# Moving one convolution tile behind the triangular inverse, on memory that the recurrence's preparation leaves

## Chip, cores and metric

The kernel runs on one core of one Trainium2 chip. The metric is the device time in microseconds (us) of one execution. Engines are called as the profile calls them: PE (TensorE), PEld (its weight loads), DVE (VectorE), ACT (ScalarE), POOL (GpSimd), SP (SyncE, which here issues nearly all DMAs).

## What is computed

One decoder layer over 1024 tokens of width 1024, in float32: a mixer, a cross-attention into 256 memory tokens and a SwiGLU, each between two RMS norms and added to the residual stream. The change lies in the mixer. One input projection feeds two groups of 512 channels; their outputs go through one output projection:

```python
p = rms_norm(x, g[0]) @ w_in_first
y_conv = conformer_conv(p[..., :2 * D_CONV], ...)   # gate, 31 taps per channel, layer norm, silu
y_rwkv, v_first = rwkv7_mix(p[..., 2 * D_CONV:], ...)
y = jnp.concatenate([y_conv, y_rwkv], axis=-1) @ w_out
```

The RWKV-7 group is a recurrence over tokens with a 64x64 state per head. The kernel runs it in chunks of 64 tokens, for which it inverts a triangular 64x64 matrix per chunk and head.

## The kernel before

**Tiling.** The tokens go in two blocks of 512 (b = 0 and 1), the 512 channels of a group in four tiles of 128 (j = 0 to 3, or four head pairs hp = 0 to 3). Each float32 matmul is done as three (`mm3`, L195 to L197) on operands split into a high and a low part. Weights are loaded raw (`wraw`), and ACT and DVE split them (`split`, L172 `whi` and L173 `wlo`); there are four raw buffers, and two each of `whi` and `wlo` at this point of the kernel.

**Stages around the change, block 0.** In the order of the code in `run`:

- `rwkv_prep(0)`, the preparation of the recurrence: decays, keys, products (`psg`, masked on DVE into `am`, L528), and bonus and gate (`bvd`, `gnd`), for head pairs 0 to 3. Its tiles are in the pool `prep0`. Its second half is asked for behind the rest of block 0's input projection.
- The memory tokens' norm (`normed(self.mem, ...)`: `xt`, the transposes `pstr`, and `ahi` and `alo`, L278 and L279). Its transposes take their PSUM from the ring `pd` of four tiles, the one from which the projections' sums `psf` come too.
- `rwkv_values(0)`, and the first panels of block 1's input projection.
- `conv_taps(0, ..., range(2))`: the convolution's tiles 0 and 1. One tile is a load `hin` (SP), one ACT activation for tap 0 and a bias (L351), and 30 dependent DVE instructions on one accumulator (L353), below called taps.
- `rwkv_inverse(0)`: loads `At`, then 31 steps of two dependent DVE instructions each (L619, L620), a way through DRAM, and small matmuls on PE.
- `rwkv_chain(0)`, the recurrence over eight chunks. Beside it lie more projection panels and the maps of the cross-attention (`memory_maps`), woven with the convolution's tiles 2 and 3 and its layer norm.
- `mix_out(0)`, the output projection, which loads what convolution and recurrence have written to DRAM (`araw<-yd`).

The order in the code is not the order on the engines. The kernel is built with `TileContext(nc, schedule_with_timeline_sim=True)`: a planner lays the instructions out on each engine when the kernel is compiled; what is asked for earlier has precedence, and what comes later fills in where it is ready. On the chip each engine then works through its list in order.

**Memory.** Pools are stacked from two sides, L and R. Tiles of one tag share a number of buffers. A pool that is opened where another was closed waits tile by tile (`reuse_waits="tile"`): a tile waits for the tiles whose place it takes. Before the change, both accumulators lie in the pool `conv0` on R, which has been open since the start, so that nothing holds them back. The pool `prep0` is the lowest on L behind the constants and weights; in it the tag `p2` (eight buffers of 2304 bytes a partition) is asked for first. An accumulator takes 2048 bytes. The memory map of the compiled kernel before shows the first `p2` buffer at the bottom of the pool; the last tile that it holds is `k` of head pair 3, which `factors(3)` reads for the last time in L514. `At` begins 8192 bytes above the bottom, behind `TT`, and its 4096 bytes reach into the buffer that holds `v` of head pair 3 last.

```python
for k in range(1, CONVW):
    nc.vector.scalar_tensor_tensor(out=a, in0=h[:, k:k + TB], scalar=w(k), in1=a, ...)
...
for t in range(31):
    ...
    nc.vector.tensor_tensor(out=w, in0=a, in1=c, op=ALU.mult)
    nc.vector.tensor_tensor(out=u, in0=u, in1=w, op=ALU.add)
```

Of the kernel before, what the change touches and what calls it, by code (L numbers as in the profile page):

```python
# [50 lines left out]
def weave(main, side, rate):  # L51

    lag = 0.0
    for us in main:
        yield us
        lag += us * rate
        while lag > 0.0:
            lag -= next(side, 1e9)
    drain(side)


def drain(*gens):
    for g in gens:
        for _ in g:
            pass


class Trunk:
# [883 lines left out]
    def run(self):  # L952
        tc = self.tc
        L, R = "left", "right"
        opened = {}

        def push(name, side):
            opened[name] = tc.tile_pool(name=name, bufs=1, side=side, reuse_waits="tile")
            return opened[name].__enter__()

        def pop(*names):
            for n in names:
                opened.pop(n).__exit__(None, None, None)
# [12 lines left out]
        kp = push("conv0", R)  # L976
# [18 lines left out]
        mk = push("mk", R)  # L995
        self.xn = 2
        self.xp = push("xb", R)
        drain(prep)
        pop("prep0")
        mT = self.pairs(mk, MEM, "m")  # L1000
        self.normed(self.mem, 0, (0, 2), mT, "g_mem", 2, (self.pd, "d"))
        self.rwkv_values(0, None)
        drain(self.w_in_block(1, h1, ev, conv_cols))

        acc = []
        drain(self.conv_taps(0, kp, kp, acc, range(2)))
        tp = push("tt0", L)
        TT = tp.tile([P, NCH * HP, CH], F32, tag="TT", name="TT")
        pp = push("inv0", L)
        self.rwkv_inverse(0, pp, TT)  # L1010
        pop("inv0")
        kv = push("kv", R)
        ka = push("conv0b", L)
# [5 lines left out]
        def conv_rest():  # L1019
            yield from self.conv_taps(0, kp, ka, acc, range(2, 4))  # L1020
            yield from self.conv_norm(0, kp, acc)
        main = chain(self.w_in_block(1, h1, ev, mix_cols[:3]), maps)
        drain(weave(main, conv_rest(), 1.0))
        pop("mix0", "gn0", "conv0b", "tt0", "kv", "xb", "mk", "conv0")
        self.filler = self.w_in_block(1, h1, ev, mix_cols[3:])

        yp = push("y0", L)
# [7 lines left out]
        kp = push("conv1", R)  # L1035
# [6 lines left out]
        acc = []  # L1042
# [20 lines left out]
        kp = push("conv1b", R)  # L1063
        acc = [kp.tile([P, TB], F32, tag="acc%d" % j, name="acc") for j in range(2)]
# [90 lines left out]
```

## Time and profile before

| | |
|---|---|
| median of 3 runs | 1613.07 us (1611.14 to 1615.81) |
| profiled execution, its own time | 1606.14 us |
| its span, first to last instruction | 1604.4 us |
| mean granted TensorE clock | 0.975 of full speed |
| PE busy | 1521.0 us (95%) |
| DVE busy | 1067.6 us (67%) |
| ACT busy | 685.9 us (43%) |

The profiled execution has a span of 1604.4 us and 1.74 us around it. Busy shares are means over stages with different limits. The PE is nearly always busy, so what counts is where it isn't, or where its clock is low. Times in the rows are microseconds from the start of the span.

### The profile page before, as it was taken

How to read it: one execution, taken by the hardware profiler on the slowest of the kernel's cores; microseconds unless marked ns; L12 is line 12 of the kernel's file. 1: busy time of each engine (PE TensorE's matmuls, PEld its weight loads, DVE VectorE, ACT ScalarE, POOL GpSimd, SP SyncE). 2: the span in 40 equal slices, each digit the busy share in tenths (PEclk: the TensorE clock that was granted, in tenths of full speed). 3: DMA queues.
4: the chain of work that ended last, by engine and by line, in shares of the span. 5: the costliest groups of instructions: out<-in, count | busy, mean ns of one | idle time of the engine just before them, and what ended most of it. 6: DMA issues, size and time to landing. Idle time of an engine off the chain costs nothing.

```text
span 1604.4 us, 22598 instructions
## 1 busy us (share of the span) xinstructions
PE 1521.0 (95%) x8688; PEld 1243.1 (77%) x8688; DVE 1067.6 (67%) x1704; ACT 685.9 (43%) x1064; POOL 57.3 (4%) x102
## 2 busy tenths in 40 slices
PE   6999699999796899899999999999999999999997
PEld 5878578888575787687888777788887888888886
DVE  6699958799689555678685997646548534444445
ACT  6554423566833344554223446434444332222222
POOL 2000000000002001000100000000002000000000
PEclk9999699999998899899999999999999999999999
DMA  6555677788646235365955444535347533333321
GB/s 219 185 168 171 197 212 250 223 284 264 217 158 203 92 99 174 99 180 172 255 160 160 148 144 149 187 119 183 92 132 244 175 102 95 94 104 92 96 88 53
DMA packets 176219, 258.41 MB, mean 161 GB/s; under 512 B 68976, under 2 KB 110064, under 8 KB 176112
## 3 DMA queue, kind: packets, MB, share of 16 engines
q1 hardware_dynamic: 175152, 256.13, 51.6%
q8 instruction: 68, 1.11, 0.3%
q10 hardware_dynamic: 960, 0.85, 0.2%
q14 instruction: 39, 0.32, 0.1%
HBM read 197.10 MB, written 59.83 MB: 160 GB/s over the span
## 4 chain that ended last, share of the span: by engine, by line
PE 78%; DVE 10%; ACT 5%; DMA 3%; issue 3%; POOL 0%; SPq 0%; DVEq 0%; ACTq 0%; POOLq 0%
PE psf L195 14%; PE psf L197 14%; PE psf L196 14%; PE pst L195 9%; PE pst L196 9%; PE pst L197 9%; DVE acc L353 4%; DVE wlo L173 1%; PE psg L525 1%; PE pstr L275 1%; ACT whi L172 1%; DVE ya L770 1%; DMA xt<-in_x_dram 1%; PE pss L702 1%; PE psq L692 1%
## 5 line engine op out<-in xcount | busy, mean ns | idle before, releaser
L172 ACT CAST whi<-wraw 128x1024 fp32r<-128x1024 f32 x256 | 268.1, 1050 | 561.9 <-PE psf L196 242.2
L173 DVE TENSOR_TENSOR wlo<-wraw,whi 128x1024 fp32r<-128x1024 f32 x256 | 312.3, 1221 | 262.4 <-ACT whi L172 258.1
L195 PE MATMUL psf<-ahi,whi 128*128 128x512 f32 (+1 forms) x1200 | 457.4, 383 | 15.6 <-ACT whi L172 10.3
L197 PE MATMUL psf<-ahi,wlo 128*128 128x512 f32 (+1 forms) x1200 | 456.8, 381 | 1.3 <-DVE wlo L173 1.2
L196 PE MATMUL psf<-alo,whi 128*128 128x512 f32 (+1 forms) x1200 | 457.3, 381 | 0.0
L195 PEld LDWEIGHTS psf<-ahi,whi 128*128 128x128 f32 x1200 | 228.6, 191 | 61.8 <-ACT whi L172 13.0
L197 PEld LDWEIGHTS psf<-ahi,wlo 128*128 128x128 f32 x1200 | 228.3, 190 | 44.6 <-DVE wlo L173 2.5
L196 PEld LDWEIGHTS psf<-alo,whi 128*128 128x128 f32 x1200 | 228.7, 191 | 41.3 <-issue 0.2
L353 DVE SCALAR_TENSOR_TENSOR acc<-hin,cols,acc 128x512 f32<-128x512 f32 x240 | 170.4, 742 | 5.8 <-ACT acc L351 5.6
L195 PE MATMUL pst<-whi,ahi 128*128 128x512 f32 x384 | 142.9, 399 | 11.3 <-ACT ahi L172 7.4
L196 PE MATMUL pst<-wlo,ahi 128*128 128x512 f32 x384 | 151.0, 395 | 0.1
L197 PE MATMUL pst<-whi,alo 128*128 128x512 f32 x384 | 146.0, 393 | 0.0
L196 PE MATMUL pst<-wlo,fhi 128*128 128x512 f32 x352 | 137.6, 392 | 0.0
L197 PE MATMUL pst<-whi,flo 128*128 128x512 f32 x352 | 134.4, 390 | 0.0
L195 PE MATMUL pst<-whi,fhi 128*128 128x512 f32 x352 | 133.8, 393 | 0.0
L195 PEld LDWEIGHTS pst<-whi,ahi 128*128 128x128 f32 x384 | 72.9, 190 | 28.4 <-ACT ahi L172 7.9
L196 PEld LDWEIGHTS pst<-wlo,ahi 128*128 128x128 f32 x384 | 73.2, 191 | 15.2 <-DVE wlo L173 0.6
L235 POOL TENSOR_TENSOR rstd<-rstd,mhalf 128x1 f32<-128x1 f32 x50 | 39.8, 804 | 1220.4 <-DVE rstd L234 1211.2
L197 PEld LDWEIGHTS pst<-whi,alo 128*128 128x128 f32 x384 | 71.9, 189 | 14.5
L919 DVE TENSOR_TENSOR ya<-pst,ya 128x512 f32<-128x512 f32 x80 | 53.9, 686 | 35.6 <-PE pst L197 35.4
L937 DVE SCALAR_TENSOR_TENSOR ftg<-ftg,psf 128x512 f32<-128x512 f32 x44 | 30.2, 686 | 70.7 <-PE psf L197 70.5
L196 PEld LDWEIGHTS pst<-wlo,fhi 128*128 128x128 f32 x352 | 66.1, 188 | 14.2 <-DVE wlo L173 0.4
(244 smaller groups left out, 1699.5 us busy)
## 6 DMA issues: line engine op xcount, KB each, us to landing
wraw<-in_w_gu_dram SPq DMA_DIRECT2D x88, 512.0 KB, 3.7
wraw<-in_w_in_dram SPq DMA_DIRECT2D x44, 512.0 KB, 4.3
wraw<-in_w_down_dram SPq DMA_DIRECT2D x44, 512.0 KB, 3.7
am<-amd SPq DMA_DIRECT2D x16, 512.0 KB, 5.7
wraw<-in_wkv_dram SPq DMA_DIRECT2D x16, 512.0 KB, 4.7
wraw<-in_w_out_dram SPq DMA_DIRECT2D x16, 512.0 KB, 4.4
wraw<-gd SPq DMA_DIRECT2D x16, 512.0 KB, 4.1
wraw<-vwd SPq DMA_DIRECT2D x16, 512.0 KB, 3.6
```

What stands on the lines that cost most here:

```text
L172: self.nc.scalar.copy(out=hi, in_=src)
L173: self.nc.vector.tensor_tensor(out=lo, in0=src, in1=hi.bitcast(F32), op=ALU.subtract)
L195: mm(ps, w[0], x[0], start=start, stop=False)
L196: mm(ps, w[0], x[1], start=False, stop=False)
L197: mm(ps, w[1], x[0], start=False, stop=stop)
L235: nc.gpsimd.tensor_tensor(r, r, self.mhalf, op=ALU.pow)
L275: nc.tensor.transpose(ps[:, t * P:(t + 1) * P], xt[:, k * P:(k + 1) * P], self.ident)
L353: nc.vector.scalar_tensor_tensor(out=a, in0=h[:, k:k + TB], scalar=w(k), in1=a, op0=ALU.mult, op1=ALU.add)
L525: nc.tensor.matmul(pg[g][:, i, :], bk[half[g], c + i, :], aq[half[g], :, c + i, :], start=True, stop=True)
L692: nc.tensor.matmul(pq[rows, j, :], S[rows, j, :], qt[rows, j, :], start=True, stop=True)
L919: nc.vector.tensor_tensor(out=y, in0=ps, in1=y, op=ALU.add)
L937: nc.vector.scalar_tensor_tensor(out=tg, in0=tg, scalar=0.5, in1=pu, op0=ALU.mult, op1=ALU.mult)
```

## The change

Tile 1's accumulator leaves the pool `conv0` (R) for a pool of its own, `conv0q`, which is opened on L when `prep0` has been closed. It takes the lowest 2048 bytes that `prep0` had. The pools that follow on L (`tt0`, `inv0`, later `conv0b`, `gn0`, `mix0`) move up by 2048 bytes, those on R that lie above `conv0` move by 2048 bytes too. Tile 1's load, its activation and its 30 taps are asked for behind `rwkv_inverse(0)` instead of ahead of it. The number of instructions stays as it is.

```diff
         drain(prep)
         pop("prep0")
+
+        kq = push("conv0q", L)
         mT = self.pairs(mk, MEM, "m")
...
         acc = []
-        drain(self.conv_taps(0, kp, kp, acc, range(2)))
+        drain(self.conv_taps(0, kp, kp, acc, range(1)))
         tp = push("tt0", L)
         TT = tp.tile([P, NCH * HP, CH], F32, tag="TT", name="TT")
         pp = push("inv0", L)
         self.rwkv_inverse(0, pp, TT)
+        drain(self.conv_taps(0, kp, kq, acc, range(1, 2)))
         pop("inv0")
...
-        pop("mix0", "gn0", "conv0b", "tt0", "kv", "xb", "mk", "conv0")
+        pop("mix0", "gn0", "conv0b", "tt0", "conv0q", "kv", "xb", "mk", "conv0")
```

## Rows read from the trace of the kernel before

**Rows 1.** The page's slices: busy tenths in 40 equal slices of the span.
```profile
PE   6999699999796899899999999999999999999997
DVE  6699958799689555678685997646548534444445
```
**Rows 2.** Windows: stretch, its length, busy us of each engine, granted clock, DMA share.
```profile
163.00:188.00 25.00, 15.52 (x59) 10.44 (x60) 24.96 (x44) 12.28 (x23) 1.74 (x4) 0.53 0.70 207
188.00:204.00 16.00, 16.00 (x83) 12.57 (x84) 15.87 (x26) 5.83 (x9) 0.52 (x1) 0.89 0.51 157
204.00:236.00 32.00, 32.00 (x181) 25.54 (x181) 15.90 (x23) 9.04 (x13) 3.80 (x6) 1.00 0.78 213
236.00:276.00 40.00, 40.00 (x182) 33.11 (x181) 36.07 (x91) 12.48 (x17) 0.00 (x0) 1.00 0.79 250
296.00:390.00 94.00, 85.36 (x936) 76.26 (x936) 85.35 (x130) 59.50 (x99) 0.00 (x0) 1.00 0.83 265
390.00:445.00 55.00, 42.65 (x353) 34.48 (x352) 41.93 (x69) 43.43 (x66) 0.00 (x0) 0.90 0.71 227
```
**Rows 3.** Waits of PE, 100 to 220: total us, times, longest.
```profile
PE psg L525 <- ACT cs L490: 5.8, 1, 5.8
PE psf L195 <- DVE alo L279: 3.7, 1, 3.7
```
**Rows 4.** Windows of the taps (L353) alone: length, DVE busy (instructions), clock.
```profile
100.00:142.00 42.00, 21.62 (x31) 1.00 0.66 198
142.00:163.00 21.00, 9.92 (x14) 1.00 0.52 164
163.00:188.00 25.00, 8.67 (x12) 0.53 0.70 207
188.00:196.00 8.00, 2.29 (x4) 0.77 0.41 120
```
**Rows 5.** Timeline of ACT at 156 and of DVE at 186: start, length, instruction.
```profile
156.74 1.28 ACT L241 ACT_TABLE_LOAD   x1 [2.58 <-DVE rn L471]
...
185.88 0.74 DVE L353 SCALAR_TENSOR_TENSOR acc<-hin,cols,acc 128x512 f32<-128x512 f32 x1
186.55 0.87 DVE L279 SCALAR_TENSOR_TENSOR alo<-pstr,cols,ahi 128x256 fp32r<-128x256 f32 x2
```
**Rows 6.** Timeline of SP's queue: loads of tiles 2 and 3.
```profile
188.10 0.32 SPq L347 DMA_DIRECT2D hin<-hd  x1
...
195.03 0.32 SPq L347 DMA_DIRECT2D hin<-hd  x1
```
**Rows 7.** Timeline of DVE: last read of `k` of head pair 3.
```profile
203.68 0.75 DVE L514 SCALAR_TENSOR_TENSOR r<-r,cols,k 128x512 f32<-128x512 f32 x1
```
**Rows 8.** Waits of SP's queue, 200 to 300.
```profile
SPq L601 <- DMA bvd<-v: 4.7, 1, 4.7
```
**Rows 9.** Timeline of DVE in the inverse: first step, some steps, last step.
```profile
236.66 0.19 DVE L619 TENSOR_TENSOR tm<-At,Tt 128x31 f32<-128x31 f32 x1 [4.04 <-DMA At<-sc]
...
245.89 0.40 DVE L619 TENSOR_TENSOR tm<-At,Tt 128x231 f32<-128x231 f32 x1
246.32 0.40 DVE L620 TENSOR_TENSOR Tt<-Tt,tm 128x231 f32<-128x231 f32 x1
246.64 0.68 DVE L327 SCALAR_TENSOR_TENSOR evh<-tg,psf 128x512 f32<-128x512 f32 x1
247.24 0.40 DVE L619 TENSOR_TENSOR tm<-At,Tt 128x240 f32<-128x240 f32 x1
...
274.78 0.22 DVE L620 TENSOR_TENSOR Tt<-Tt,tm 128x31 f32<-128x31 f32 x1
```
**Rows 10.** Timeline of DVE at the recurrence's end: last state, last output.
```profile
426.97 0.42 DVE L704 TENSOR_TENSOR Sn<-pss,Sn 128x256 f32<-128x256 f32 x1
...
444.13 0.69 DVE L740 TENSOR_TENSOR Y<-Y,bv 128x512 f32<-128x512 f32 x1
```
**Rows 11.** Waits of PE, 440 to 470.
```profile
PE pst L195 <- ACT ahi L172: 7.4, 1, 7.4
```

## The prediction

> **What bounds the kernel now.** I began with the page's slices. The PE is full nearly everywhere, so a change to DVE work can pay only where the PE is not full: here in slice 5 (160 to 200 us) and in slices 11 and 13 [rows 1]. The accumulators of the change belong to the first of these places, so I cut it with windows. From 163 to 188 the PE is busy 15.52 of 25 us, at a mean clock of 0.53, while DVE is busy 24.96 of 25 [rows 2]. The PE's list of waits says what it lacks there: once ACT (5.8 us, `cs`) and once DVE (3.7 us, `alo` of the memory norm, which holds the ring of sums that the next projection panel needs) [rows 3]. So in this stretch DVE sets the pace. From 204 to 236 the picture is turned round: the PE is full, and DVE is busy 15.90 of 32 us. From 236 to 276, while the inverse runs, it is busy 36.07 of 40, and beside the recurrence (296 to 390) 85.35 of 94 [rows 2].
>
> Who fills DVE from 163 to 188? The taps alone take 8.67 us of it, 12 instructions; 14 lie from 142 to 163, 4 from 188 to 196 [rows 4]. They are the lowest in precedence of all that is asked for there, and the stretch is where work is late. Both tiles run alternately: tile 2's load, which needs tile 0's `hin`, goes out at 188.10, and tile 3's, which needs tile 1's, at 195.03, so both end within 7 us of each other [rows 6]. One tap in front of the instruction on which the PE waits can be seen: at 185.88, ahead of `alo` at 186.55 [rows 5].
>
> Behind this stretch two things run. The PE's stream of panels goes on full until the recurrence begins. The recurrence ends later than the stream has work for: its last state comes at 426.97, its last output at 444.13 [rows 10], the PE is busy 42.65 of 55 us from 390 to 445 [rows 2], and then it waits 7.4 us for the recurrence's part of `mix_out`'s input [rows 11]. So a gain ahead of the inverse counts for the total only as far as it reaches the recurrence's end.
>
> **The change part by part.** Durations are those of the profiled execution.
>
> *Taps taken out of the full stretch.* With tile 1 away, tile 0's 30 taps take the slots alone. By 142 there were 31 [rows 4], so tile 0 should be done at about 145, and from 163 to the release of the PE 11 taps are gone (12 less the one behind 186.55): 11 x 8.67/12 = 7.9 us. Bounds: if tile 0, whose taps wait for one another, spreads over the same stretch and keeps half the slots, 4.0 us; if the taps ahead of `rn` that delay ACT's table load at 156.74 (it idled 2.58 us for it [rows 5]) go as well, 7.9 + 2.2 (three taps of 0.72) = 10.1. I take 7.9.
>
> *The same from 188 to 204.* Four taps (2.29 us [rows 4]) and the sum of the two accumulators leave a DVE that is busy 15.87 of 16 [rows 2], ahead of the last factors of the preparation. The PE is full there too, so between 0 and 2.3 us; I take 1.5.
>
> *When tile 1 can start.* Its accumulator takes the bottom of `prep0`, so it waits for `k` of head pair 3, last read at 203.68 [rows 7] (about 194 after the gains above), and not for the preparation's last stores: `At`, which lies on `v`'s buffer, waited for that one's store (`bvd`) 4.7 us [rows 8], as it will after the change, since `At` moved by 2048 bytes still covers it. `hin` has a buffer free from the start.
>
> *Taps put into the idle stretch.* From `k`'s last read to the inverse's first step DVE has 32 - 15.90 = 16.1 us idle [rows 2], room for 22 taps of 0.72. They hide under a full PE, but some stand in front of preparation work on the way to `At`: some nine DVE instructions of the last head pairs, half of which meet a tap half done, 9 x 0.5 x 0.36 = 1.6 us. Bounds 0 and 3.2; I take 1.5.
>
> *Taps left for the inverse.* Eight remain. The inverse's two instructions per step depend on each other, and the planner puts whatever is ready between them. What one costs can be read at 246: from 245.89 to 246.32 the pitch is 0.43, so the next step was due at 246.75; with `evh` (0.68) in between it came at 247.24, 0.49 late [rows 9]. A tap (0.74, as at 185.88 [rows 5]) would cost 0.55, eight 4.4 us. But DVE idles 40 - 36.07 = 3.9 us in that stretch [rows 2], in which some hide. Bounds 0.5 and 4.4; I take 2. [...]
>
> *Nothing else.* The load, activation and taps are the same in number. SP's queue has tile 1's load behind the inverse's in precedence, but it needs nothing that is late. The moved pools at 204 and later stand on tiles that were freed earlier than they are asked for, `At` aside. Tiles 2 and 3 wait for the inverse's memory as before.
>
> *Sum.* At the inverse's end: -7.9 - 1.5 + 1.5 + 2.0 = -5.9 us. The recurrence and `mix_out` behind it move by the same amount, since the PE's stream, which moves by some 8, stays ahead. The profiled execution would come to 1606.14 - 5.9 = 1600.2 us (span 1598.5). The runs' median lies 6.9 us above this execution; I put the difference on it: 1613.07 - 5.9 = 1607.2 us.
>
> **The rivals.**
>
> *The stall stays.* ACT's chain and the transposes at half clock, not DVE's queue, set the PE's restart at 187: then taking the taps out leaves DVE idle and the PE waiting. For it: the longest wait in [rows 3] is on ACT, and the PE itself works at clock 0.53 there [rows 2]. Against it: DVE idles 0.04 of 25 us, and at the restart it is DVE that the PE waits for. At most ACT's 2.2 us would be won, against 1.5 + 2 lost later: 1613 + 1.3, about 1614 us, or the gain goes into the PE's idle time ahead of `mix_out`; no change.
>
> *The inverse pays (the slower one).* Tile 1's taps have precedence over block 1's later panels and alternate with the inverse. If they start late, as they would if the accumulator were held until the store that `At` awaits, only about 5 us x 1/0.72 = 6 fit ahead of the first step at 236.66 [rows 9], and 24 lie in the inverse: 24 x 0.55 = 13.2 us, and the 1.5 in the preparation, against the 9.4 won: +5.3, so 1618.4 us. It decides from (9.4 - 1.5)/0.55 = 14 taps in the inverse on. For it: the alternation is seen at 246 [rows 9]; against it: `k`'s last read at 203.68 is 33 us ahead of the inverse.
>
> *The clock recovers.* The PE drops from 2.4 to about 1.2 GHz in the stall (granted 0.53, and 0.89 from 188 to 204 [rows 2]) after it has waited. If the shorter stall keeps it up, 16 x 0.11 = 1.8 us of the restart come back, and at most half of the 15.52 us busy (7.3 at 0.53): -7.7 to -13.2, so 1605 to 1600 us. In the Trainium skill, page "TensorE: Matmul & The Clock Gate", section "Terms", the penalty is the throttled time times the share of pulses withheld. By that the two stretches would hold 25 x 0.47 + 16 x 0.11 = 13.5 us to win, which is more than the rows allow, since the PE stood still for 9.5 us of them.
>
> *The change doesn't do what it says:* the planner already spaces both tiles by what is ready, and tile 0 fills all slots that tile 1 leaves. Then 0 us.
>
> **How the numbers follow.** What a measurement of this kernel can tell from no change is 0.3%, here 4.8 us. Chances: the sum as forecast 0.55 (its own range, by the bounds of the first term, is -2.0 to -8.1, 1605 to 1611 us; 0.43 of it beyond 0.3%, 0.12 within); the clock's extra gain 0.05; the stall stays 0.20; the change doesn't do it 0.03; the inverse pays 0.17. That makes faster 0.48, same 0.35, slower 0.17. The range goes from 1600 (the gains' upper bounds, 10.1 + 2.3 with nothing paid back but 0.5, are 11.9 us, and with the clock's least 13.7) up to 1616.5, where part of the slower case begins; about 1 in 10 is left out on each side.
>
> **What would show it.** Right: no taps between 150 and 190; PE busy more than 18 of the 25 us there, its restart (first `psf` behind the memory norm) near 179 instead of 187; `k`'s last read near 194 and tile 1's taps from then to about 235; the inverse's last step near 269 instead of 275, the last output near 438. Wrong: taps of tile 0 up to 180 (the first term), a restart that doesn't move (the stall stays), more than 14 taps between the inverse's first and last step (the slower case), or an inverse that ends at 269 and a last output still at 444, in which case the gain is lost beside the recurrence, whose DVE is nearly full.

## The result, and the profile after

The changed kernel is slower: 1627.34 us (median of 4 runs) against 1614.39 us (median of 4 runs of the kernel before), ratio 1.0088, 95% interval 1.0071 to 1.0105 (ratios, here and below, are those on record; the quotient of two medians can differ from them by up to 0.0008). Three executions among the runs below, with a mean granted clock of 0.65 to 0.74 and 19 to 37% more time, are left out of medians and ratios. The profiled execution of the changed kernel took 1626.74 us with a span of 1625.0 us, so it stands near its median. The one of before (1606.14 us) lies 8 us below its own median. Differences between the two traces therefore come out larger (20.6 us of span) than those between the medians (13 us).

The windows of [rows 2], and behind them the taps alone (their line, L353; length, DVE busy, clock), whose first three stretches are those of [rows 4]:
```profile
163.00:188.00 25.00, 19.81 (x86) 14.42 (x86) 22.05 (x36) 16.61 (x28) 2.68 (x5) 0.73 0.62 189
188.00:204.00 16.00, 16.00 (x95) 12.98 (x94) 11.40 (x16) 5.69 (x8) 0.00 (x0) 1.00 0.65 172
204.00:236.00 32.00, 32.00 (x178) 26.36 (x177) 21.07 (x37) 8.34 (x11) 4.66 (x6) 1.00 0.93 258
...
390.00:445.00 55.00, 38.29 (x381) 28.76 (x375) 40.24 (x73) 30.97 (x49) 0.00 (x0) 0.74 0.45 144
```
```profile
100.00:142.00 42.00, 19.94 (x27) 1.00 0.69 208
142.00:163.00 21.00, 2.53 (x4) 1.00 0.66 207
163.00:188.00 25.00, 0.00 (x0) 0.73 0.62 189
...
204.00:228.00 24.00, 2.24 (x3) 1.00 0.92 258
228.00:304.00 76.00, 20.19 (x27) 1.00 0.76 242
```
The reader is to see two halves. Up to 204 the change does what was forecast: no tap stands between 163 and 188, the PE is busy 19.81 us there instead of 15.52 [rows 2], and at a higher clock (0.73, not 0.53). From 204 on it doesn't: ahead of the inverse DVE is filled little more than before (13.55 of the 24 us from 204 to 228, 12.01 before; the 21.07 of 32 in the window above hold the first steps of the inverse), 3 taps lie ahead of the inverse and 27 in it.

The timeline says how that comes. First the stretch in which tile 1 might have started and the one in which it did (DVE and ACT), then the inverse's first and last instruction and, from its middle, one step with all that lies between its two instructions:
```profile
195.37 0.75 DVE L514 SCALAR_TENSOR_TENSOR r<-r,cols,k 128x512 f32<-128x512 f32 x1
...
220.23 0.69 ACT L554 ACTIVATE cs<-pspr,cols 128x512 f32<-128x512 f32 x1 [2.27 <-DVE v L552]
220.81 0.81 ACT L351 ACTIVATE acc<-hin,convb,cols 128x512 f32<-128x512 f32 x1
...
221.65 0.75 DVE L353 SCALAR_TENSOR_TENSOR acc<-hin,cols,acc 128x512 f32<-128x512 f32 x1
...
228.38 0.19 DVE L619 TENSOR_TENSOR tm<-At,Tt 128x31 f32<-128x31 f32 x1
...
241.98 0.32 DVE L619 TENSOR_TENSOR tm<-At,Tt 128x156 f32<-128x156 f32 x1
242.22 1.22 DVE L173 TENSOR_TENSOR wlo<-wraw,whi 128x1024 fp32r<-128x1024 f32 x1
243.35 0.74 DVE L309 SCALAR_TENSOR_TENSOR evq<-psf,cols,evq 128x511 f32<-128x511 f32 x1
244.01 0.74 DVE L353 SCALAR_TENSOR_TENSOR acc<-hin,cols,acc 128x512 f32<-128x512 f32 x1
244.67 0.22 DVE L312 SCALAR_TENSOR_TENSOR evq<-carry,cols,evq 128x1 f32<-128x1 f32 x1
244.80 0.32 DVE L620 TENSOR_TENSOR Tt<-Tt,tm 128x156 f32<-128x156 f32 x1
...
303.47 0.21 DVE L620 TENSOR_TENSOR Tt<-Tt,tm 128x31 f32<-128x31 f32 x1
```
`k` is read for the last time at 195.37, 8.3 us earlier than before [rows 7]. Tile 1's activation comes 25 us later, directly behind `L554`, the preparation's last instruction on ACT, and with no wait listed in front of it: the trace shows nothing on the chip that held it, it stands there in ACT's program. The inverse then starts 8.3 us earlier than before [rows 9] and ends 28.7 us later (303.47 against 274.78): it takes 75 us instead of 38. In the step shown, the second instruction starts 2.82 us behind the first (0.43 in the step of [rows 9] with nothing between), and only one of the four instructions between them is a tap.

What lies in DVE between the inverse's first and last step, by line; first the kernel before, then the changed one (busy us, mean ns; the last column is idle time before them):
```profile
L619 DVE TENSOR_TENSOR tm<-At,Tt 128x31 f32<-128x31 f32 (+15 forms) x31 | 10.6, 341 | 4.7 <-DMA At<-sc 4.0
...
L173 DVE TENSOR_TENSOR wlo<-wraw,whi 128x1024 fp32r<-128x1024 f32 x7 | 8.6, 1222 | 1.5 <-ACT whi L172 1.3
```
```profile
L173 DVE TENSOR_TENSOR wlo<-wraw,whi 128x1024 fp32r<-128x1024 f32 x19 | 23.2, 1224 | 3.9 <-ACT whi L172 3.9
L353 DVE SCALAR_TENSOR_TENSOR acc<-hin,cols,acc 128x512 f32<-128x512 f32 x27 | 20.2, 748 | 0.0
L619 DVE TENSOR_TENSOR tm<-At,Tt 128x31 f32<-128x31 f32 (+15 forms) x31 | 10.6, 341 | 0.4
...
L832 DVE TENSOR_TENSOR kvl<-psf,kvh 128x256 fp32r<-128x256 f32 x7 | 2.9, 418 | 0.0
```
The inverse's own work is the same (31 steps; 10.6 us for the first instructions of all of them). The taps bring 20.2 us. Beside them 19 splits of weight panels (`wlo`) lie in the stretch instead of 7, which is 14.6 us more, and 7 evacuations of the memory's projections (`kvl`, 2.9 us, the last of them directly behind the last step) that before came behind it. The PE runs on with its panels while the inverse lasts, and each panel asks DVE for a split and evacuations: the longer the inverse takes, the more of them it has to let through.

Behind the inverse the delay goes on. The recurrence's end, for [rows 10], and the PE's wait ahead of `mix_out`, for [rows 11]:
```profile
448.70 0.42 DVE L704 TENSOR_TENSOR Sn<-pss,Sn 128x256 f32<-128x256 f32 x1
...
464.12 0.69 DVE L740 TENSOR_TENSOR Y<-Y,bv 128x512 f32<-128x512 f32 x1
```
```profile
PE pst L195 <- ACT ahi L172: 5.9, 1, 5.9
```
The last state is 21.7 us later than before, the last output 20.0 us (464.12 against 444.13), and the span 20.6 us longer. The whole loss is there when the recurrence ends; behind it nothing is added, and the PE's wait ahead of `mix_out` is no longer than before (5.9 us, 7.4 in [rows 11]). The PE has run out of other work by then: from 390 to 445 it is busy 38.29 us (42.65 before) at a clock of 0.74.

### The profile page after: what moved, and what is told of

The parts are those of the page before. It is cut to its first block, busy times and chain, and to the rows that moved or that the text cites. A ratio compares the mean times of both kernels' runs of the same rounds, so it can differ in the third digit from the quotient of the medians.

```text
span 1625.0 us, 22615 instructions
## 1 busy us (share of the span) xinstructions
PE 1527.2 (94%) x8688; PEld 1249.2 (77%) x8688; DVE 1069.1 (66%) x1704; ACT 686.3 (42%) x1064; POOL 57.8 (4%) x102
## 4 chain that ended last, share of the span: by engine, by line
PE 79%; DVE 9%; ACT 4%; DMA 4%; issue 3%; SPq 0%; POOL 0%; DVEq 0%; ACTq 0%; POOLq 0%
PE psf L195 15%; PE psf L197 14%; PE psf L196 14%; PE pst L195 9%; PE pst L196 9%; PE pst L197 9%; DVE acc L353 3%; PE psg L525 1%; DVE wlo L173 1%; PE pstr L275 1%; DVE ya L770 1%; PE pspr L439 1%; DMA vwd<-evw 1%; DMA xt<-in_x_dram 1%; ACT whi L172 1%
## 5 line engine op out<-in xcount | busy, mean ns | idle before, releaser
L353 DVE SCALAR_TENSOR_TENSOR acc<-hin,cols,acc 128x512 f32<-128x512 f32 x240 | 173.1, 749 | 12.1 <-ACT acc L351 11.4
L196 PEld LDWEIGHTS pst<-wlo,fhi 128*128 128x128 f32 x352 | 66.1, 188 | 14.2 <-DVE wlo L173 0.4
```

What stands on the lines that cost most here:

```text
L196: mm(ps, w[0], x[1], start=False, stop=False)
```

## The experiments

Each was timed beside the kernel before on the same chip; ratios are to that. Its median was 1610.12 us beside the runs of the order alone, of no taps, of the first hold and of tile 1 beside the recurrence; 1610.93 beside the memory alone, half the taps, the second hold and GpSimd; and 1611.20 beside the three with late taps. "Inverse" is from the start of its first step on DVE to that of its last, "last output" the last `Y` of the first block's recurrence, both in the profiled execution (before: 38.1 us and 444.13). Two executions of one program differ in these places too: the first run below has the program of the kernel before, and its last output came at 451.53. Differences of some us in the last output prove nothing by themselves; the medians decide.

**The order alone.** The tile is asked for behind the inverse, but its accumulator stays in `conv0`.
```
-        drain(self.conv_taps(0, kp, kp, acc, range(2)))
+        drain(self.conv_taps(0, kp, kp, acc, range(1)))
...
         self.rwkv_inverse(0, pp, TT)
+        drain(self.conv_taps(0, kp, kp, acc, range(1, 2)))
```


> Only the order is changed: tile 1 is asked for behind the inverse, but its accumulator stays in the pool conv0, which is open from the start. Theory (late memory: the accumulator on the preparation's memory is held until the preparation's last instructions are out, so that 27 of its taps fall into the inverse): the taps run as before, alternating with tile 0's, all 60 done before the inverse begins; the inverse takes 38 us and the time is that of before, 1614 us within 5. Rival (order: whoever is asked for behind the inverse alternates with it, wherever its memory lies): some 27 taps in the inverse, 75 us for it, and about 1627 us.

Measured: 1610.72 us, ratio 1.0008 (0.999 to 1.0025); inverse 37.7 us, without a tap; the PE is busy 14.78 of 25 us from 163 to 188. The planner puts all taps where they were: on DVE and ACT the trace has the same instructions in the same order as the kernel before, from the first to the last. The order does nothing by itself. As one program in two executions, the two traces also show how far such traces lie apart: this one's granted clock was 0.85 from 296 to 330 (1.00 in the trace before) and its last output 7.4 us later.

**The memory alone.** The accumulator lies in the recurrence's memory, but the tile is asked for ahead of the inverse, as before.
```
         drain(self.conv_taps(0, kp, kp, acc, range(1)))
+        drain(self.conv_taps(0, kp, kq, acc, range(1, 2)))
...
         self.rwkv_inverse(0, pp, TT)
-        drain(self.conv_taps(0, kp, kq, acc, range(1, 2)))
```


> Tile 1's accumulator lies in the recurrence's memory as in the change, but the tile is asked for ahead of the inverse, as before. Theory (the memory decides, the order does nothing): tile 1's activation comes behind the preparation's last instructions (near 221), some 27 taps lie between the inverse's first and last step, 1625 to 1630 us, as the change. Rival (both edits are needed): tile 1 starts near 195, at most 10 taps in the inverse, 1605 to 1613 us.

Measured: 1626.99 us, ratio 1.0094 (1.0078 to 1.0109); inverse 75.5 us, last output 465.72. ACT's timeline in this run:
```profile
220.67 0.69 ACT L554 ACTIVATE cs<-pspr,cols 128x512 f32<-128x512 f32 x1 [2.27 <-DVE v L552]
221.25 0.81 ACT L351 ACTIVATE acc<-hin,convb,cols 128x512 f32<-128x512 f32 x1
```
The activation stands behind the same instruction as in the changed kernel, although the tile is asked for earlier; in all, PE, DVE and ACT have the same instructions in the same order as in the changed kernel, so that this is a second measurement of its program (16 us slower than the kernel before). With the run before, this settles it: the memory makes the loss and sets the start; the order has no part in it.

**No taps.** The changed kernel without tile 1's 30 taps (its convolution is left out).
```
-            for k in range(1, CONVW):
+            for k in range(1, 1 if (b, j) == (0, 1) else CONVW):
```


> The changed kernel without tile 1's 30 taps (load and activation stay; the convolution of 128 channels in block 0 is left out but for its first tap). Theory: what is lost lies in these taps alone, so the inverse is back at about 38 us with 7 splits of weights in it, the PE's restart stays at its early place, the recurrence begins some 8 us earlier than before, and the time is 1614 - 6 = 1608 us (1602 to 1612). Rival (moved pools: the shift by 2048 bytes makes new waits): the loss stays, 1620 us or more. Rival (nothing to win: the early restart of the PE is given back at the recurrence): 1614 us.

Measured: 1600.14 us, ratio 0.9944 (0.9929 to 0.996); PE 19.76 of 25 us from 163 to 188, inverse 40.0 us, last output 441.67. That is below the forecast (1602 to 1612). The moved pools do no harm, and freeing the full stretch is worth some 9 us if the taps cost nothing elsewhere. From here to the changed kernel it is 0.0144 in the ratio, 23 us, for 30 taps of 0.75 us on DVE (22 us). The inverse is longer by 35 us (75.1 against 40.0). Without the taps the planner also laid out other instructions in another order, so the comparison holds more than the taps' removal; no run keeps the rest in place.

**Half the taps.** The changed kernel with tile 1's taps 16 to 30 left out.
```
-            for k in range(1, CONVW):
+            for k in range(1, 16 if (b, j) == (0, 1) else CONVW):
```


> The change with 15 of tile 1's 30 taps left out (its convolution is cut short there); 3 taps ahead of the inverse and 12 in it, against 27 and none. Theory (a tap costs its 0.75 us divided by the share of DVE that the panels' splits and evacuations leave, about 0.6, so 1.25 us): the inverse takes 40 + 12 x 1.25 = 55 us, the whole 1610 to 1616 us, half way between the change and the one with no taps of tile 1. Prediction's price (0.55 us per tap): the inverse 40 + 6.6 = 47 us, 1603 to 1607 us.

Measured: 1608.35 us, ratio 0.999 (0.9977 to 1.0003); 12 taps in the inverse, which takes 57.6 us (227.97 to 285.59); last output 445.13. Two lines of DVE's groups in the inverse:
```profile
L173 DVE TENSOR_TENSOR wlo<-wraw,whi 128x1024 fp32r<-128x1024 f32 x13 | 15.9, 1223 | 3.2 <-ACT whi L172 3.0
...
L353 DVE SCALAR_TENSOR_TENSOR acc<-hin,cols,acc 128x512 f32<-128x512 f32 x12 | 8.9, 744 | 0.0
```
None, 12 and 27 taps go with 7, 13 and 19 splits and with 40.0, 57.6 and 75.1 us: 1.47 us for each of the first 12 taps, 1.30 over all 27. The price that I had forecast, 0.55, would have given 47 us here. The time follows less evenly than expected: against no taps, 12 taps lengthen the inverse by 17.6 us, but the kernel loses 7 to 8 us by ratios and medians, and in the two traces the last output comes 3.5 us later only: the recurrence, whose first state comes 19.6 us later (327.88 instead of 308.32), has its last only 4.8 us later (429.12 instead of 424.28). So a delay of the inverse isn't paid in full: here the inverse ends 14.2 us later, in the changed kernel 32.0 us, and the last output comes 3.5 and 22.5 us later, so that in these traces the recurrence took up some 10 us each time. The time itself lies between the forecast by theory (1610 to 1616) and that by the prediction's price (1603 to 1607), and missed both.

**A start at `k`'s last read.** The order's edit, with the accumulator in `conv0`, and the first activation made to wait for the instruction that reads `k` last: its bias is added to a product of that result with zero.
```
             nc.vector.scalar_tensor_tensor(out=r, in0=r, scalar=self.col("r_k", hp), in1=k, op0=ALU.mult, op1=ALU.mult)
+            if (b, hp) == (0, 3):
+                self.cbq = self.sp.tile([P, 1], F32, tag="cbq", bufs=1, name="cbq")
+                nc.vector.scalar_tensor_tensor(out=self.cbq, in0=r[:, 0:1], scalar=0.0, in1=self.cb[:, 1:2],
+                                               op0=ALU.mult, op1=ALU.add)
...
-            nc.scalar.activation(out=a, in_=h[:, 0:TB], func=AF.Identity, scale=w(0), bias=self.cb[:, j:j + 1])
+            nc.scalar.activation(out=a, in_=h[:, 0:TB], func=AF.Identity, scale=w(0),
+                                 bias=self.cbq if (b, j) == (0, 1) else self.cb[:, j:j + 1])
```


> Tile 1 is asked for behind the inverse with its accumulator in conv0, and its first activation takes its bias from a column that is made from the result of L514 of head pair 3 (one DVE instruction on one column more): the start at k's last read that the prediction took for given. Theory: some 24 taps lie between that read and the inverse, 6 in it. If the prediction's own sum held for such a start, 1614 - 6 = 1608 us. If the inverse is stretched by each tap and by the splits that slip in beside it, at twice the taps' own time, 6 taps cost 8 us and the time is 1612 to 1616 us. Rival (order): slower than before by 10 us or more, since the taps are still asked for behind the inverse.

Measured: 1632.44 us, ratio 1.0141 (1.0118 to 1.0165), slower than the changed kernel itself. The forecast fell, but the run held a second thing: the new column moved later pools by 32 bytes. It was made again with the same hold written into a column that exists:
```
             nc.vector.scalar_tensor_tensor(out=r, in0=r, scalar=self.col("r_k", hp), in1=k, op0=ALU.mult, op1=ALU.mult)
+            if (b, hp) == (0, 3):
+                nc.vector.scalar_tensor_tensor(out=self.cb[:, 1:2], in0=r[:, 0:1], scalar=0.0, in1=self.cb[:, 1:2],
+                                               op0=ALU.mult, op1=ALU.add)
```


> Repeats the hold at k's last read (accumulator in conv0, first activation behind the last head pair's r times k), but the hold writes a column that exists already, so that no pool moves. In the first version of it a new column moved later pools by 32 bytes, and behind 600 us the 128x512 matmuls of the projections took 396 ns instead of 389. Theory (that move cost some 10 of the 22 us): 389 ns again, last output near 460, 1619 to 1625 us: still slower than before, since a start at k's last read fills DVE ahead of the inverse and splits that were put off land in it (inverse 48 to 52 us instead of 38). Rival (the hold itself costs all of it): 1630 to 1634 us. Prediction's own reading (a start at 194 is harmless): 1604 to 1609 us.

Measured: 1619.40 us, ratio 1.0051 (1.0034 to 1.0068); inverse 53.1 us, last output 456.41. PE, DVE and ACT have the same instructions in the same order in both versions, so that 13 us of the first version's loss came from the moved pools (the last section has the rows). What is left answers the question of the prediction: tile 1 starts when the prediction had it start, and the kernel is still slower than before. (The tile is asked for behind the inverse here; the hold with the old order wasn't run.) DVE's timeline at the hold, and the windows around the inverse:
```profile
196.36 0.15 DVE L516 SCALAR_TENSOR_TENSOR convb<-r,convb 128x1 f32<-128x1 f32 x1
197.39 3.12 DVE L353 SCALAR_TENSOR_TENSOR acc<-hin,cols,acc 128x512 f32<-128x512 f32 x4 [0.89 <-ACT acc L351]
```
```profile
163.00:188.00 25.00, 20.39 (x90) 15.06 (x90) 21.43 (x35) 15.97 (x28) 2.24 (x5) 0.73 0.61 183
...
204.00:236.00 32.00, 32.00 (x173) 25.76 (x172) 30.51 (x50) 8.67 (x11) 3.96 (x6) 1.00 0.81 218
```
The "idle" 16 us from 204 to 236 [rows 2] are filled (up to 228, ahead of the inverse, DVE is busy 22.83 of 24 us, 12.01 before), and 6 taps are left for the inverse. It takes 13 us more than without taps all the same, because 12 splits stand in it instead of 7 (6.1 us), beside the taps (4.4) and 4 evacuations (`kvl`, 1.7). So idle time ahead of the inverse wasn't free here: the taps come before the panels' splits, and what is put off lands between the steps. A further part is lost behind the inverse: from its last step to the recurrence's first state it is 44 us (282.97 to 327.13), against 35 before (274.78 to 309.54). Half the taps shows 42, the order alone 37. Why is not settled; the PE is busy 23.29 of 24 us from 276 to 300, so it may be that the recurrence's first products stand behind panels in the PE's program.

**Beside the recurrence.** Tile 1 joins tiles 2 and 3 in `conv0b`, behind the inverse.
```
-        kq = push("conv0q", L)
...
-        drain(self.conv_taps(0, kp, kq, acc, range(1, 2)))
...
-            yield from self.conv_taps(0, kp, ka, acc, range(2, 4))
+            yield from self.conv_taps(0, kp, ka, acc, range(1, 4))
```


> Tile 1 joins tiles 2 and 3 beside the recurrence, its accumulator in the pool conv0b that takes the inverse's memory: the preparation's stretch is relieved as in the change, the inverse has no taps, but DVE beside the recurrence has 90 taps instead of 60. Theory: the inverse takes about 38 us and ends some 8 us earlier than before; the 21.6 us of taps must fit into the 22 us that DVE idles from 296 to 445, so the convolution's norm ends later: between 1608 us (all hidden) and 1625 us (the convolution becomes the last input of mix_out). Rival (moved pools): slower although the inverse is short.

Measured: 1625.28 us, ratio 1.0098 (1.0075 to 1.0122); inverse 39.1 us, last output 439.30, no later than before. But the convolution's last output comes at 463.0 (436.6 before, 444.0 with the order alone), and `mix_out` waits for them:
```profile
PE pst L195 <- ACT ahi L172: 17.8, 1, 17.8
```
DVE's work beside the recurrence was 85.35 of 94 us [rows 2] already; 22 us more of it make the convolution the last of `mix_out`'s inputs.

**On GpSimd.** The kernel before with tile 1's taps as a product and a sum on GpSimd.
```
             for k in range(1, CONVW):
-                nc.vector.scalar_tensor_tensor(out=a, in0=h[:, k:k + TB], scalar=w(k), in1=a,
-                                               op0=ALU.mult, op1=ALU.add)
+                if (b, j) == (0, 1):
+                    t = pool.tile([P, TB], F32, tag="t", bufs=2, name="tapq")
+                    nc.gpsimd.tensor_scalar(out=t, in0=h[:, k:k + TB], scalar1=w(k), scalar2=None, op0=ALU.mult)
+                    nc.gpsimd.tensor_tensor(out=a, in0=a, in1=t, op=ALU.add)
+                else:
+                    nc.vector.scalar_tensor_tensor(out=a, in0=h[:, k:k + TB], scalar=w(k), in1=a,
+                                                   op0=ALU.mult, op1=ALU.add)
```


> The kernel before, with tile 1's 30 taps on GpSimd (a product and a sum each, 60 instructions of 128x512), its accumulator in conv0. Theory (the loss is VectorE's time alone): DVE free of tile 1 in both places, no taps in the inverse, inverse 39 to 41 us, 1598 to 1604 us, faster than both kernels. Rivals: GpSimd takes over 1.5 us an instruction and tile 1's input is held so long that tile 3 starts late (last convolution output behind 445): 1610 to 1630 us; or DVE's own instructions get longer while GpSimd runs (taps over 0.80 us): 1605 to 1615 us.

Measured: 1615.86 us, ratio 1.0032 (1.002 to 1.0045), slower and not faster than before, so that the theory fell. GpSimd is busy 24.84 of 25 us from 163 to 188, and DVE's groups of 160 to 240 (first this run, then the kernel before) show what that does:
```profile
L533 DVE TENSOR_TENSOR am<-psg,gmask 128x512 f32<-128x512 f32 x12 | 8.0, 680 | 3.2 <-PE psg L530 3.2
L514 DVE TENSOR_TENSOR bkp<-k,s 64x512 f32<-64x512 f32 x4 | 4.5, 1130 | 0.0
L173 DVE TENSOR_TENSOR bhl<-r,bhl 128x512 fp32r<-128x512 f32 x3 | 3.6, 1205 | 0.0
L517 DVE TENSOR_TENSOR aqp<-r,Dx 128x512 f32<-128x512 f32 x2 | 3.5, 1761 | 0.0
```
```profile
L528 DVE TENSOR_TENSOR am<-psg,gmask 128x512 f32<-128x512 f32 x12 | 8.1, 684 | 2.3 <-PE psg L525 2.3
L509 DVE TENSOR_TENSOR bkp<-k,s 64x512 f32<-64x512 f32 x4 | 2.7, 683 | 0.0
...
L173 DVE TENSOR_TENSOR bhl<-r,bhl 128x512 fp32r<-128x512 f32 x3 | 2.1, 685 | 0.0
...
L512 DVE TENSOR_TENSOR aqp<-r,Dx 128x512 f32<-128x512 f32 x2 | 1.4, 681 | 0.0
```
Products of two tiles in SBUF go from 683 to 1130 ns (`bkp`), from 685 to 1205 (`bhl`), and from 681 to 1761 (`aqp`); `am`, which reads its first operand from PSUM, keeps its 680. The taps that stay on DVE, which read two tiles in SBUF as well, go from 743 to 828 ns in the mean (100 to 480), which is the rival that the forecast named for this. The preparation ends later (inverse from 241.31). The Trainium skill, page "SBUF — State Buffer", section "SBUF: two separate sides", says that a VectorE instruction with two inputs in SBUF and a GpSimd instruction that reads SBUF exclude each other for a whole instruction's length. The rows agree.

**Only the last taps late.** The order's edit; tile 1 begins as before, and only its last 15 (or 11) taps wait for `k`'s last read, by the same product with zero, put on the weight of the first of them. A third run holds the 15 to one head pair earlier.
```
             nc.vector.scalar_tensor_tensor(out=r, in0=r, scalar=self.col("r_k", hp), in1=k, op0=ALU.mult, op1=ALU.mult)
+            if (b, hp) == (0, 3):
+                wq = self.cwh[:, CONVW + 16:CONVW + 17]
+                nc.vector.scalar_tensor_tensor(out=wq, in0=r[:, 0:1], scalar=0.0, in1=wq, op0=ALU.mult, op1=ALU.add)
```


> The kernel before, but only the last 15 taps of tile 1 (16 to 30) are held until k's last read of the fourth head pair; accumulator in conv0, no tap in the inverse. Theory (what is moved must fit into DVE's idle 16 us ahead of the inverse and may put off few splits): PE busy 18.5 to 20 of 25 us from 163 to 188, the inverse starts at 230 to 234 and takes 39 to 44 us, the whole 1602 to 1608 us, faster than both kernels. Rival (any tap that is late puts off the panels' splits, so that the inverse pays it back): the inverse takes over 46 us, 1609 to 1615 us.

> The same with the last 11 taps of tile 1 held (20 to 30). Theory: less is taken out of the full stretch and less is put ahead of the inverse: PE busy 17.5 to 19.5 of 25 us from 163 to 188, inverse 39 to 42 us, 1602 to 1608 us. Rival (the taps up to the hold still stand in the full stretch, nothing is gained): PE below 16.5 there, 1609 to 1612 us.

> The last 15 taps of tile 1 held until k's last read of the third head pair, one head pair earlier (some 10 us). Theory: the taps begin before DVE's idle stretch, part of them still ahead of the last head pair's factors: PE from 163 to 188 as with the later hold, the inverse starts 1 to 3 us later than with the later hold, 1603 to 1610 us. Rival (an earlier start is better, since nothing is left near the inverse): 1600 to 1604 us.

Measured: 1609.88 us, ratio 0.9995 (0.9981 to 1.0008); 1608.26 us, 0.9981 (0.9968 to 0.9994); 1609.40 us, 0.9989 (0.9977 to 1.0001). The first two miss the forecast time (1602 to 1608), the third lies in its range (1603 to 1610). With 15 late taps the PE is busy 20.65 of 25 us from 163 to 188 and the inverse takes 42.0 us (233.75 to 275.73), about as forecast (18.5 to 20, 39 to 44). But that is 3.9 us longer than before, so it ends no earlier (274.78 before), and what the PE has won it waits for ahead of `mix_out`: 18.07 us, against 7.41 before and 8.20 with the order alone:
```profile
447.95 0.79 PE L195 MATMUL pst<-whi,ahi 128*128 128x512 f32 x1 [18.07 <-ACT ahi L172]
```
With 11 late taps two fifths of the early gain are there (PE 17.64, 15.52 before) and 0.2% of the time. Held one head pair earlier, the inverse starts 0.8 us later (234.54) than with the later hold and takes 41.4 us. None of the three is faster by the 0.3% that can be told; no version with all taps was found that is.

## Why the prediction was wrong, step by step

- *Taps out of the full stretch, 7.9 us, and 188 to 204, 1.5 us:* right. Together with the 1.5 us paid back in the preparation, 7.9 us were forecast at the inverse's first step; 8.3 were measured (228.38 against 236.66). `k`'s last read, forecast near 194, came at 195.37; the PE's restart, forecast near 179, at 177.77. That the size fits to 0.4 us is in part luck: in the four other runs that take the taps out of this stretch and put none of them ahead of 200, the first step came 5.2 to 8.7 us earlier than before. The PE's higher clock in the stall (0.73) came with it; the rival that gave it a gain beyond this has no room in the 8.3 us.
- *When tile 1 can start:* the step that failed first. I took it for a question of when the memory comes free on the chip (last read of `k`), and it was one of where the instruction stands in its engine's program. With the accumulator in `conv0` the same tile starts at 196.54 when held to `k`'s last read; with it in the recurrence's memory it stands behind the preparation's last instruction on ACT, at 220.8 and 221.3, whatever the order in which it is asked for. Nor did a later tile of the preparation hold the place until then: the last ones, `v` and `cs` of head pair 3, are stored at 220.22 and 220.94 (2.9 us each until they land), so the activation at 220.81 would have come too early for either. That the planner plans a tile on a closed pool's memory only behind all instructions of that pool fits both runs, but is my reading of them.
- *Taps put into the idle stretch, 22 of them for 1.5 us:* 3 stood there. And had the rest stood there too, the price was wrong: in the repeated hold, with 6 taps in the inverse and 24 ahead of it, the inverse ends 8.2 us later than before (282.97), where the sum had it 5.9 earlier.
- *Taps left for the inverse, 8 at 0.55 us:* 27 at 1.3 us. The rows that I priced them by [rows 9] show one instruction in one gap, and what it adds to the next step. They don't show the steady demand beside the chain: the PE's panels ask for splits while it lasts, so a longer stretch holds more of them (20.2 us of taps and 14.6 us of splits make up the 35 us by their length; no run took the splits out). With the measured price the sum closes: 27 x 1.3 = 35 us, less the 8.3 won, is 26.8 us at the inverse's end; 28.7 were measured, and the 1.9 us between are those by which the inverse without taps is longer than before (40.0 against 38.1). That is bookkeeping and no test, since the price is taken from the same two traces.
- *"The recurrence and `mix_out` move by the same amount":* only in part. The recurrence starts 29.7 us later than before and ends 20.0 us later (from first to last state it takes 109.5 us instead of 117.4); with half the taps it starts 18.3 us later and ends 1.0 us later. What it takes up is likely DVE work that had been done inside the longer inverse, which no run separates. And [rows 11] was misread: the 7.4 us end with the load of the convolution's part, not of the recurrence's. SP, ACT and PE of the kernel before, at that place:
```profile
438.91 2.45 SPq L749 DMA_DIRECT2D araw<-yd  x2
442.66 1.37 ACT L172 CAST ahi<-araw 128x512 fp32r<-128x512 f32 x2 [1.46 <-DMA araw<-yd]
443.33 0.79 PE L195 MATMUL pst<-whi,ahi 128*128 128x512 f32 x1 [7.41 <-ACT ahi L172]
448.03 0.87 SPq L749 DMA_DIRECT2D araw<-yd  x2
```
  The first two loads wait for the convolution's stores, the last two for the recurrence's; ACT reaches `ahi` 1.5 us before the first of them is there. So convolution and recurrence end close to each other, and a gain that reaches the recurrence alone would not have brought `mix_out` forward; in the runs with the tile beside the recurrence and with 15 late taps the PE waits there for 17.8 and 18.1 us.
- *The range and the rivals:* the rival "the inverse pays" was the right one, with the right condition (an accumulator held until the preparation's end) and nearly the right count (24 taps). Its price was that of the failed step, so it came to 1618.4, and the range, cut at 1616.5, missed 1627.34. At 1.3 us per tap the same rival gives 24 x 1.3 = 31 and 1.5 against 9.4 won: 23 us at the inverse's end. "The stall stays" and "does nothing" fell.
- *Profiled execution and median:* I put 6.9 us between them on the forecast. The execution of before was a short one, with the recurrence at a full clock (the order alone, the same program, had 0.85 from 296 to 330); that of after wasn't short, and so 20.6 us between the traces are 13 between the medians.

## What to carry to other kernels

Work that is slipped into a chain of dependent instructions on a shared engine costs more than its own length when another engine, never idle, keeps feeding that engine: price it from the whole stretch (length per instruction added), not from one gap, and expect idle time just ahead of the chain to cost too, where that engine's requests are served in it. When a tile gets other memory, ask not only when the last reader is done, but where the writer will stand in its engine's program; on reused memory that can be behind everything the old pool did. And before moving work out of a full stretch, add up every place where it can go: here each of them (inverse, stretch ahead of it, recurrence, GpSimd) gave back what the full stretch won.

## What the runs showed of the hardware

- *A shift of 32 bytes.* In the first version of the hold, the pools behind the new column lie 32 bytes higher; by the compiled kernels' memory maps, which no trace shows, the projections' activations `ahi` and `alo` of the later panels are among them, `whi` and `wlo` are not. Their matmuls from 1100 to 1600, in that run and in the repeated one:
```profile
L196 PE MATMUL psf<-alo,whi 128*128 128x512 f32 x377 | 150.1, 399 | 0.0
L195 PE MATMUL psf<-ahi,whi 128*128 128x512 f32 x377 | 149.5, 398 | 2.2 <-ACT whi L172 2.2
```
```profile
L196 PE MATMUL psf<-alo,whi 128*128 128x512 f32 x384 | 150.2, 392 | 0.0
L195 PE MATMUL psf<-ahi,whi 128*128 128x512 f32 x384 | 149.8, 392 | 2.2 <-ACT whi L172 2.2
```
  At a granted clock of 1.00 in both, each of them is 6 to 7 ns longer, and the whole 13 us (1632.44 against 1619.40). They also follow each other more slowly: from start to start it is 234 instead of 227 ns in the median (600 to 1600). Beside the column that the hold writes, the two kernels differ in these places alone; which operand's place does it was not separated. One column of four bytes per partition cost more than the hold that it was made for (1619.40 against 1610.93).
- *GpSimd beside VectorE.* A 128x512 product on GpSimd took 2075 ns and a sum 1661 ns in the mean, with VectorE busy beside it, and VectorE's instructions with two SBUF operands took up to 2.6 times their length beside them (`aqp`, 1761 ns against 681).
